# State-space side work in five lanes, eighteen groups of seven products, and cache products on GpSimd

## The chip, the cores and the metric

One core of a Trainium2 chip runs the whole program in one launch. The metric is the device time of that core in microseconds (us); lower is better. The kernel before takes 1260.09 us, the median of three runs (1259.04 to 1262.6). Engines: TensorE (PE in the profile, its weight loads PEld) multiplies matrices, VectorE (DVE) and ScalarE (ACT) do elementwise work, GpSimd (POOL) does some elementwise work and issues DMAs, SyncE (SP) issues most DMAs.

## The reference, cut to what matters

One step of a decoder layer with two branches: attention over a sliding window, and a diagonal state-space model (S5). 528 prompt tokens (16 meta tokens and 512) and 8 sample tokens go through the same weights.

```python
h = rmsnorm(x) @ w_in                    # 2048 -> 8704 columns
q, k, v, z_a, u, z_s, g_a, g_s = split(h)   # 1024, 256, 256, 1024, 1024, 1024, 2048, 2048
o = window_attention(rope(norm(q)), rope(norm(k)), v)  # 16 query heads on 4 key heads, window 128
# state space: 64 groups of 16 channels, 64 complex states each
bu = b_bar @ u                           # per group and token
h_t = lam_bar * h_(t-1) + bu_t           # scan over the tokens
y = gelu(real(c @ h) + d * u);  y = y * sigmoid(y @ w_glu + b_glu)
br_a = (o * silu(z_a)) @ w_attn_out
br_s = (y * silu(z_s)) @ w_ssm_out
out = x + (sigmoid(g_a) * br_a + sigmoid(g_s) * br_s) @ w_out
```

For each sample token attention runs over a cache of 16 meta and 127 window positions and the token itself: scores are a product of the cached keys with the query, summed over 64 dimensions; the output is a product of the cached values with the weights, summed over 144 positions. Updated caches and states are outputs too. All is float32.

## The kernel before, in words

**Products.** A float32 product is made from split operands: each weight unit (128 x 1024) is loaded as `raw`, rounded by ScalarE to `whi`, and VectorE computes the remainder `wlo` (L1019 and L1020); a product is whi·xh + whi·xl + wlo·xh, three matmuls for each 128 rows. The 536 token columns are held in two halves of 268, of which gates and queries use 260. A *block* is 128 output columns of `w_in` for all tokens: two weight units, 16 row tiles, three matmuls and two column halves, 96 matmuls (`mm`, L1168).

A *group* (`quad`, L1419, with `Quads` for its weights) makes two blocks from seven half-sized products instead of eight, by forming sums of weight units on VectorE (L1084) and sums of inputs (`tau`) once: 7 x 8 x 3 = 168 matmuls instead of 192. `NQ` says how many groups there are, and `NA` how many plain blocks stand ahead of them. `XORDER` and `ORDER1` fix the order of the 48 gate blocks (g_s, z_s, z_a, g_a) and of the u, k and v blocks.

**Order of the program.** Start with norms and five blocks; four plain blocks; `NQ` groups (four of them, `QHEADS`, make the queries); the ordered blocks of `ORDER1` ("x" a gate block, "u" one eighth of u, "h" one of the four k and v blocks); the gate blocks left over (`while nx < 47`, L1719); gate block 47 by hand; eight half-blocks of the gated unit product, w_glu on Y1 (L1746); sixteen half-blocks of the state-space output product on Y2 (L1762); `bg.drain()`; the attention-output product on A (L1780); w_out in groups.

**Side work.** Everything else is written as generators and put into `Background` (L963). The products call `bg.step(budget)` after every few row tiles (`GRAIN` 2 in the state-space stage, so a step is 12 matmuls; 4 in attention, 24 matmuls). A step adds budget to a credit; the generators are run in turn, lane by lane; what they yield is taken off the credit (roughly us of VectorE), and `yield None` takes the lane out for the rest of this step, so that a later instruction is issued a step later. With `fair` off (in attention) the first lane runs as long as it can and the others get the rest. This fixes the order of the program; the framework then orders each engine's queue by its own estimate of times, with weight splits and evictions at high priority. Matmuls of side work are issued behind the last product (`issue_after`).

**State-space stage.** It begins with the first "u" block. Lane 1 runs `ssm_consts` for eight units (128 channels each): scaled copies on ScalarE, four tables on VectorE, and at its end the tap product `kp` whose result goes through memory into the matrices T (L417 to L427). Lane 0 runs `ssm_block` for each unit: the bu product (L478), its products with the table straight out of PSUM into p1 and p2 (L492, L493), the combination, the scan, the way back, and the output product (L534, L537), then the gelu and six stores to `yD` (L556). The loads of U (12 DMAs, `ssm_load`) are issued on GpSimd's queue when a unit is done.

**Attention.** `attention()` follows in lane 0 when the eighth unit is done: values, keys, then for 4 key heads a rope of the queries and 4 blocks each of scores, softmax, transposes and weighing. The sample tokens are a lane of their own, added at that point: `sample_heads` gathers their rows, `sample_weigh` loads the key cache and the value cache in 16 pieces each (`cache`, two buffers), multiplies each piece by the query or the weights and sums it, both on VectorE (L659, L660). Last, `Attn.sample` loads that output and the gate (`zs`, in the tile `dV` of attention, L922), transposes and multiplies them into `oT`; then `attended()` splits `oT` into the operands A of the attention-output product (L1712).

## Time and profile before

| | us |
|---|---|
| median of three runs | 1260.09 |
| lowest and highest | 1259.04, 1262.6 |
| the profiled execution's own time | 1259.92 |
| its span in the trace | 1258.1 |
| TensorE busy | 1245.8 |
| VectorE busy | 986.4 |
| ScalarE busy | 632.5 |
| GpSimd busy | 324.4 |

A row of the views names line, engine, operation, output and inputs by the program's names, shapes and count, then the busy time, the mean duration in ns, and the idle time of the engine before it with what ended it. A matmul's recorded duration (283 ns for 260 columns) overlaps the next; what counts is how many start in a stretch. A wait is put down to what came last. The chain of waits runs backwards from the last instruction, so its rows are the work that set the time.

### The profile page before, as it was taken

Reading aid. Unit: us, or ns where it says so; the run is one execution under the profiler, and the core shown is the slowest. Engines: PE = TensorE matmul, PEld = TensorE weight load, DVE = VectorE, ACT = ScalarE, POOL = GpSimd, SP = SyncE. Lnnn points to the kernel's source line nnn. Section 1 sums busy time; section 2 is a strip of 40 time slices with the busy share of each in tenths; the row PEclk is TensorE's granted clock in tenths of the full one; section 3 lists DMA queues with packets and bytes.
Section 4 is the critical chain, followed back from the end, with each engine's and each line's share of the span. In section 5 each row is a group of like instructions: output and inputs, shape, how many; then the busy total and the mean of one; then the engine's idle time right before and its main releaser. Section 6 shows DMA issues by size and latency. Waiting matters only on the chain.

```text
span 1258.1 us, 26470 instructions
## 1 busy us (share of the span) xinstructions
PE 1245.8 (99%) x10333; PEld 1221.6 (97%) x10333; DVE 986.4 (78%) x1516; ACT 632.5 (50%) x1351; POOL 324.4 (26%) x541
## 2 busy tenths in 40 slices
PE   9999999999999999999999999999999999999998
PEld 9999999999999999999999999999999899999998
DVE  8687878888898756778689858899987477887875
ACT  8554444444445587555552233657665433344342
POOL 0003999940000015337345132112111000000000
PEclk9999999999999999999999999999999999999999
DMA  8544443444464475557556479777667466555441
GB/s 294 198 162 149 138 144 110 143 127 162 153 195 154 144 241 175 176 167 180 170 145 173 124 232 278 244 218 230 215 201 240 151 195 190 166 186 168 143 138 51
DMA packets 99872, 222.42 MB, mean 177 GB/s; under 512 B 17324, under 2 KB 36868, under 8 KB 99716
## 3 DMA queue, kind: packets, MB, share of 16 engines
q1 hardware_dynamic: 86500, 191.97, 47.3%
q0 software_dynamic: 13248, 28.77, 8.9%
q8 instruction: 81, 1.33, 0.4%
q14 instruction: 43, 0.35, 0.1%
HBM read 183.17 MB, written 38.43 MB: 176 GB/s over the span
## 4 chain that ended last, share of the span: by engine, by line
PE 89%; issue 4%; DMA 3%; DVE 2%; POOL 1%; ACT 1%; SPq 0%; DVEq 0%; ACTq 0%; POOLq 0%
PE mm L1179 41%; PE pr L1415 37%; PE mm L1271 2%; PE wg L865 1%; PE aux L1415 1%; PE aux L1179 1%; DMA cache<-in_kc 1%; PE aux L1271 1%; DMA KH<-KH 1%; PE wg L537 1%; PE tr L537 1%; PE aux L816 1%; DMA qD<-x 1%; PE tr L478 0%; PE aux L817 0%
## 5 line engine op out<-in xcount | busy, mean ns | idle before, releaser
L1085 ACT CAST whi<-raw 128x1024 fp32r<-128x1024 f32 x168 | 173.2, 1049 | 167.8 <-DVE raw L1084 68.9
L1086 DVE TENSOR_TENSOR wlo<-raw,whi 128x1024 fp32r<-128x1024 f32 x168 | 206.7, 1251 | 56.4 <-ACT whi L1085 56.0
L1019 ACT CAST whi<-raw 128x1024 fp32r<-128x1024 f32 (+3 forms) x124 | 118.4, 964 | 147.1 <-PE mm L1179 70.7
L1415 PE MATMUL pr<-tau,whi 128*128 128x260 f32 x992 | 180.1, 283 | 0.0
L1179 PE MATMUL mm<-xh,whi 128*128 128x260 f32 (+1 forms) x744 | 172.8, 286 | 0.2 <-ACT xr L1244 0.2
L1179 PE MATMUL mm<-xh,wlo 128*128 128x260 f32 (+1 forms) x744 | 172.2, 285 | 0.0
L1179 PE MATMUL mm<-xl,whi 128*128 128x260 f32 (+1 forms) x744 | 171.8, 285 | 0.0
L1020 DVE TENSOR_TENSOR wlo<-raw,whi 128x1024 fp32r<-128x1024 f32 (+3 forms) x124 | 137.6, 1118 | 32.6 <-ACT whi L1019 32.1
L1415 PE MATMUL pr<-cb,whi 128*128 128x260 f32 x848 | 153.0, 283 | 0.0
L1415 PEld LDWEIGHTS pr<-tau,whi 128*128 128x128 f32 x992 | 152.7, 188 | 0.0
L1415 PE MATMUL pr<-tau,wlo 128*128 128x260 f32 x496 | 139.4, 282 | 0.0
L1415 PEld LDWEIGHTS pr<-cb,whi 128*128 128x128 f32 x848 | 130.8, 188 | 0.2 <-ACT z L1449 0.2
L1179 PEld LDWEIGHTS mm<-xh,whi 128*128 128x128 f32 x744 | 123.6, 188 | 1.6 <-issue 1.2
L1179 PEld LDWEIGHTS mm<-xl,whi 128*128 128x128 f32 x744 | 123.8, 188 | 0.4 <-issue 0.4
L1179 PEld LDWEIGHTS mm<-xh,wlo 128*128 128x128 f32 x744 | 123.4, 188 | 0.2 <-issue 0.2
L1084 DVE TENSOR_TENSOR raw<-raw 128x1024 f32<-128x1024 f32 x95 | 118.7, 1250 | 1.4
L1415 PE MATMUL pr<-cb,wlo 128*128 128x260 f32 x424 | 119.1, 283 | 0.2 <-DVE wlo L1086 0.2
L1415 PE MATMUL pr<-xl,whi 128*128 128x260 f32 x376 | 105.1, 282 | 0.0
L1415 PE MATMUL pr<-xh,wlo 128*128 128x260 f32 x376 | 105.0, 283 | 0.0
L1179 PE MATMUL mm<-Y,whi 128*128 128x260 f32 x576 | 104.4, 287 | 0.3 <-ACT t L1755 0.3
L1415 PE MATMUL pr<-xh,whi 128*128 128x260 f32 x376 | 104.3, 284 | 0.0
L1415 PEld LDWEIGHTS pr<-tau,wlo 128*128 128x128 f32 x496 | 93.1, 188 | 0.0
(432 smaller groups left out, 3022.9 us busy)
## 6 DMA issues: line engine op xcount, KB each, us to landing
raw<-in_w SPq DMA_DIRECT2D x202, 512.0 KB, 4.4
gD<-z SPq DMA_DIRECT2D x36, 260.0 KB, 3.1
t<-gD SPq DMA_DIRECT2D x32, 260.0 KB, 3.4
cache<-in_vc POOLq DMA_DIRECT2D x16, 286.0 KB, 3.4
cache<-in_kc POOLq DMA_DIRECT2D x15, 288.0 KB, 4.8
xr<-in_x SPq DMA_DIRECT2D x16, 268.0 KB, 6.0
xg<-in_x SPq DMA_DIRECT2D x8, 536.0 KB
sbw<-rawD SPq DMA_DIRECT2D x16, 260.0 KB, 6.8
```

Source lines behind the costliest of these rows:

```text
L537: nc.tensor.matmul(o[n], lhsT=D["CL"][:, 2 * e + n, i, 1:5], rhs=H[:, 2 * e + n, i, 0:140], start=False, stop=(i == 1))
L816: nc.tensor.matmul(ps[:, e, 0:272], lhsT=q, rhs=KH[:, k0:k0 + 272], start=True, stop=False)
L865: nc.tensor.matmul(pv[64 * e:64 * e + 64, 0:256], lhsT=V, rhs=pr[:, e::2], start=(i == 0), stop=(i == len(parts) - 1))
L1019: nc.scalar.copy(out=hi, in_=raw)
L1020: self.dve = nc.vector.tensor_tensor(out=lo, in0=raw, in1=hi.bitcast(F32), op=ALU.subtract).ins
L1084: nc.vector.tensor_tensor(out=o, in0=o, in1=i, op=ALU.add)
L1085: nc.scalar.copy(out=hi, in_=t)
L1086: self.dve = nc.vector.tensor_tensor(out=lo, in0=t, in1=hi.bitcast(F32), op=ALU.subtract).ins
L1179: m = nc.tensor.matmul(ps[:, c, 0:W], lhsT=wt[:, k], rhs=xo(kt, c), start=f, stop=l)
L1271: nc.tensor.matmul(ps[:, c, 0:260], lhsT=wt[:, kt % 8], rhs=xk(xo, kt, c, 8), start=f, stop=l)
L1415: m = nc.tensor.matmul(bank, lhsT=wt[:, p], rhs=x(p, e), start=first and f and p == 0, stop=l and p == 7, skip_group_check=not first and l ...
```

## The change: lanes, order, engines, groups

- `NQ` goes from 16 to 18. The order of the gate blocks follows it, so four blocks fewer are left for the loop ahead of block 47 (six instead of ten).
- `ORDER1` starts with two u blocks and ends with two x blocks.
- `Background` has five lanes, and its turn goes on where it stopped for want of credit. `BUDGET` falls from 6.4 to 5.6.
- The tap product and what follows leave `ssm_consts` for a generator of their own, `ssm_taps`, in lane 4. Loads of U and stores of y leave `ssm_block` for `transfers()`, in lane 2; a store is issued four steps after its unit.
- A wrapper `InOrder` keeps GpSimd's DMAs and products of this work in program order.
- bu is copied from PSUM by ScalarE into the place in `H` where the states come later, and VectorE multiplies from there with four wide products.
- The sample tokens' generator starts in lane 3 once the norms of the heads are known; its part on the caches waits for attention's keys, and it also runs `Attn.sample`, whose tile is now one of the cache's buffers.
- The products of cache pieces go to GpSimd; the sums stay on VectorE, a step later. The copy of the sink into `S` goes from GpSimd to ScalarE.
- Attention also waits for all units and their stores; `NDELAY` goes from 4 to 6 steps.

```diff
+class InOrder:
+    def __init__(self, tc, nc):
+        self.tc, self.nc, self.gpsimd = tc, nc, self
+    def dma_start(self, **kw):
+        return self.tc.keep_in_program_order(self.nc.gpsimd.dma_start(**kw))
+    def tensor_tensor(self, **kw):
+        return self.tc.keep_in_program_order(self.nc.gpsimd.tensor_tensor(**kw))
...
 def ssm_consts(...):
-    D["CL"] = CL
+    D["CL"], D["tab"] = CL, tab
     yield 1.4
+    behind(ssm_taps(nc, pool, dram, R, D, ub, bb, CL, e32, d_skip, later))
+
+def ssm_taps(nc, pool, dram, R, D, ub, bb, CL, e32, d_skip, later):
     yield None
+    yield None
+    while "kp" not in R:
+        yield None
...
     nc.gpsimd.dma_start(out=kD, in_=k0)
+    yield 0.3
+    yield None
+    yield None
     for j in range(4):
         nc.gpsimd.dma_start(out=R["T"][ub % 2]...)
...
+    R["ready"] = ub
 def ssm_block(...):
+    Hu = H[:, :, :, 9:9 + NC]
...
-                v.tensor_tensor(out=p1[:, i, a], in0=bi, in1=bc(tab[:, 0, a], 2, NB), op=ALU.mult)
-                v.tensor_tensor(out=p2[:, i, a], in0=bi, in1=bc(tab[:, 1, a], 2, NB), op=ALU.mult)
+                nc.scalar.copy(out=Hu[:, a, i], in_=b[:, :, 0:NC])
...
-        yield 2.2
+    yield 0.6
+    for i in range(2):
+        for j, p in ((0, p1), (1, p2)):
+            v.tensor_tensor(out=p[:, :, i], in0=hu[:, :, i], in1=bc(tab[:, j], 2, NB), op=ALU.mult)
+        yield 1.4
...
+    def store():
...
+    R["ys"].append([store, 4 if ub < 7 else 1])
 def sample_heads(...):
+    for _ in range(4):
+        yield None
 def sample_weigh(...):
-            v.tensor_tensor(out=t, in0=t, in1=by, op=ALU.mult)
+            nc.gpsimd.tensor_tensor(out=t, in0=t, in1=by, op=ALU.mult)
+            yield None
             v.tensor_reduce(out=out[:, c * n:(c + 1) * n], in_=t, axis=AX.X, op=ALU.add)
-            yield 1.5
-            for _ in range(CWAIT):
-                yield None
+            yield 0.8
 class Attn:
-        nc.gpsimd.tensor_copy(out=S[:, :, 144], in_=C["sink"][:, 4 * kv:4 * kv + 4])
+        nc.scalar.copy(out=S[:, :, 144], in_=C["sink"][:, 4 * kv:4 * kv + 4])
...
-        o = pool.tile([P, 2, 64], F32, name="o_s", tag="sv")
+        o = pool.tile([P, 576], F32, name="ozs", tag="cache")
+        zs = o[:, 128:192].rearrange("p (b c j) -> p b c j", b=8, c=2)
+        o = o[:, 0:128].rearrange("p (n d) -> p n d", n=2)
...
-        zs = pool.tile([P, 8, 2, 4], F32, name="zs", tag="dV", bufs=1)
...
-BUDGET = 6.4
+BUDGET = 5.6
-NDELAY = 4
+NDELAY = 6
-NA, NQ = 4, 16
+NA, NQ = 4, 18
-ORDER1 = [(k, 0) for k in "xuhuhuhuhuxuxuxu"]
+ORDER1 = [(k, 0) for k in "uuxuhuhuhuhuxuxx"]
 class Background:
-        ways = list(self.lanes)
+        n = self.first if self.fair else 0
+        ways = self.lanes[n:] + self.lanes[:n]
...
-                if not q or self.credit <= 0:
+                if self.credit <= 0:
+                    self.first = [w is q for w in self.lanes].index(True)
+                    break
+                if not q:
                     continue
...
+    def transfers():
+        nonlocal loaded
+        S["ys"] = []
+        while loaded < 7 or done < 8 or S["ys"]:
+            ub = loaded + 1
+            for y in S["ys"]:
+                y[1] -= 1
+            if S["ys"] and S["ys"][0][1] < 0:
+                S["ys"].pop(0)[0]()
+            elif ub in uDs and ub < done + 2:
+                yield None
+                yield None
+                ssm_load(pn, S["U"][ub % 2], uDs.pop(ub))
+                loaded = ub
+            yield None
     def ssm(ub):
-        while ready < ub:
+        while min(S.get("ready", -1), loaded) < ub:
             yield None
...
     def finish():
             normed.append(1)
+            bg.add(samples(), lane=3)
     def samples():
+        for _ in range(6):
+            yield None
         qk = yield from sample_heads(...)
         smp.extend(qk)
+        while not (at and at.keyed):
+            yield None
         smp.extend((yield from sample_weigh(...)))
+        while not at.gated(3):
+            yield None
+        yield from at.sample(smpl, smp[2])
+        smp.append(True)
...
+            bg.add(transfers(), lane=2)
...
     def attention():
-        while not normed:
+        while not normed or done < 8 or S["ys"]:
             yield None
...
-        bg.add(samples(), lane=2)
...
+        at.keyed = True
...
-        while len(smp) < 3:
+        while len(smp) < 5:
             yield None
-        yield from at.sample(smp[2])
```

More of the change, by code (lines that the diff above doesn't have):

```diff
@@ L334, in ssm_states, with ssm_consts @@
     yield 2.5
-def ssm_consts(nc, pool, dram, R, D, ub, a_bT, a_bN, a_cT, e32, d_skip, later, free):
+def ssm_consts(nc, pool, dram, R, D, ub, a_bT, a_bN, a_cT, e32, d_skip, later, free, behind):
     v = nc.vector
@@ L940 @@
 NUNIT = 176
-CWAIT = 1
 GRAIN = 2
-BUDGET = 6.4
+BUDGET = 5.6
 GBUDGET = 0.5
@@ L1308, in trunk @@
     sp, Ds = None, {}
-    ready, done, uDs = -1, 0, {}
+    loaded, done, uDs = -1, 0, {}
+    pn = InOrder(tc, nc)
     def ssm_sets():
-        nonlocal ready
         for ub in range(8):
             Ds[ub] = {}
-            yield from ssm_consts(nc, sp, dram, S, Ds[ub], ub, A["bT"], A["bN"], A["cT"], e32, dsk,
-                                  lambda: tc.issue_after(bg.last), lambda: ub - 2 not in Ds)
-            ready = ub
-    def load_u():
-        for ub in sorted(uDs):
-            if ub < done + 2:
-                ssm_load(nc, S["U"][ub % 2], uDs.pop(ub))
+            yield from ssm_consts(pn, sp, dram, S, Ds[ub], ub, A["bT"], A["bN"], A["cT"], e32, dsk,
+                                  lambda: tc.issue_after(bg.last), lambda: ub - 2 not in Ds, lambda g: bg.add(g, lane=4))
+    def transfers():
[13 more added lines that the diff above has]
+            yield None
     def ssm(ub):
         nonlocal done
-        while ready < ub:
+        while min(S.get("ready", -1), loaded) < ub:
             yield None
-        yield from ssm_block(nc, sp, S, Ds[ub], ub, yD[ub], lambda: tc.issue_after(bg.last))
+        yield from ssm_block(pn, sp, S, Ds[ub], ub, yD[ub], lambda: tc.issue_after(bg.last))
         del Ds[ub]
         done = ub + 1
-        load_u()
     rawD = dram.tile([12, 2, P, 2, CH], F32, name="rawD")
@@ L1367, in sums @@
             else:
-                if "ax" not in S:
-                    S["ax"] = aux.tile([P, 2, 512], F32, name="aux")
                 ps = S["ax"][:, 1, P:]
@@ L1613, in trunk @@
                 nc.gpsimd.memset(t, 0.0)
-            S["ax"] = S.get("ax") or aux.tile([P, 2, 512], F32, name="aux")
-            S["bu"] = [aux.tile([P, 512], F32, name=n) for n in ("tr", "wg")] + [S["ax"][:, 0]]
-            S["kp"] = S["ax"][:, 1, 0:P]
             bg.add(ssm_states(nc, sc, sp, S, A["h0"]), lane=1)
             bg.add(ssm_sets(), lane=1)
+            bg.add(transfers(), lane=2)
             grain[0] = GRAIN
@@ L1623, in trunk @@
             v.tensor_tensor(out=uf, in0=ps, in1=R_, op=ALU.mult)
+        if n == 0:
+            S["ax"] = aux.tile([P, 2, 512], F32, name="aux")
+            S["bu"] = [aux.tile([P, 512], F32, name=nm) for nm in ("tr", "wg")] + [S["ax"][:, 0]]
+            S["kp"] = S["ax"][:, 1, 0:P]
         uD = dram.tile([P, 2 * CH], F32, name="uD", bufs=8)
-        nc.gpsimd.dma_start(out=uD, in_=flat(uf))
+        pn.dma_start(out=uD, in_=flat(uf))
         uDs[n] = uD
-        load_u()
         bg.add(ssm(n))
@@ L1654, in attention @@
         nc.gpsimd.memset(C["neg"], NEG)
-        at = Attn(nc, ap, aux, dram, C, oT, gD[24:32], rawD, rkD, rqD, lambda: tc.issue_after(bg.last))
+        at = Attn(pn, ap, aux, dram, C, oT, gD[24:32], rawD, rkD, rqD, lambda: tc.issue_after(bg.last))
         vals = [at.values(e) for e in range(2)]
```

47 lines of the change are left out of this document (25 added, 22 removed).

## Prediction

> **What bounds the kernel now.** I read the page's busy line and its chain first, then the busy time by stage, then the chain in order of time.
>
> ```profile
> PE 1245.8 (99%) x10333; PEld 1221.6 (97%) x10333; DVE 986.4 (78%) x1516; ACT 632.5 (50%) x1351; POOL 324.4 (26%) x541
> PE 89%; issue 4%; DMA 3%; DVE 2%; POOL 1%; ACT 1%; SPq 0%; DVEq 0%; ACTq 0%; POOLq 0%
> ...
> 113.40:437.50 324.10, 324.10 (x2700) 321.31 (x2699) 275.18 (x309) 155.06 (x219) 146.62 (x202) 1.00 0.45 146
> 437.50:740.00 302.50, 302.50 (x2559) 298.27 (x2558) 224.89 (x441) 161.10 (x495) 128.32 (x245) 1.00 0.59 171
> 740.00:999.50 259.50, 253.70 (x2065) 238.17 (x2064) 207.97 (x395) 147.71 (x402) 47.88 (x85) 1.00 0.73 228
> 999.50:1092.20 92.70, 92.65 (x770) 92.50 (x771) 69.27 (x90) 33.32 (x38) 0.19 (x1) 1.00 0.58 181
> ```
>
> In the stage rows the columns after the length are TensorE, its weight loads, VectorE, ScalarE and GpSimd, then granted clock, DMA share, GB/s. TensorE is the bound everywhere, at clock 1.00. The stages are: groups of seven products (113.4 to 437.5), ordered blocks with the state-space work (to 740), attention under the remaining products (to 999.5), then the attention-output product. Only 740 to 999.5 has visible TensorE idle: 259.50 - 253.70 = 5.8 us. So a gain must come from fewer matmuls or from those 5.8 us; a loss comes if side work no longer ends under its cover.
>
> ```profile
> 327.65 20.35 PE pr L1415 x168
> ...
> 992.05 0.91 POOL zs L924
> 995.41 2.73 DMA zs<-gD
> 998.82 0.63 ACT A L1698
> 999.55 92.65 PE mm L1179 x768
> ```
>
> ```profile
> 999.55 1.20 PE L1179 MATMUL mm<-A,whi 128*128 128x260 f32 x6 [2.43 <-ACT A L1698]
> ```
>
> The first row is one whole group, the last the plain product without side work: 92.65 / 768 = 0.1206 us a matmul. Between them is the end of the side work: the sample rows' gate `zs` loads only after attention's last weighing, and the split of A waits for it; TensorE stands 2.43 us.
>
> **Term 1, eighteen groups.** A group replaces two plain blocks: 2 x 96 x 0.1206 = 23.16 us against 20.35, so 2.81 saved; two more groups save 5.6 us. Their extra weight sums lie on VectorE, which the group stage leaves 49 us idle in 324 while TensorE never stops; I cost them at nothing. Were that cover short, it would show as idle in the stage that now has none.
>
> **Term 2, less cover.** Groups now end near 437.5 + 2 x 20.35 = 478, and four plain blocks (46.3 us) leave the stretch in which side work runs. Its end, now the last product before 996.9, moves to about 991.4. So 559 us of cover become 513. What must fit:
>
> ```profile
> L1020 DVE TENSOR_TENSOR wlo<-raw,whi 128x1024 fp32r<-128x1024 f32 x79 | 96.4, 1221 | 27.2 <-ACT whi L1019 26.7
> L659 DVE TENSOR_TENSOR cache<-cache,qv 128x576 f32<-128x576 f32 x16 | 12.1, 755 | 4.1 <-DMA cache<-in_kc 4.0
> L659 DVE TENSOR_TENSOR cache<-cache,ssc 128x572 f32<-128x572 f32 x16 | 11.6, 749 | 0.0
> L1216 DVE TENSOR_TENSOR z<-mm,R 128x520 f32<-128x520 f32 x14 | 9.7, 693 | 4.6 <-PE mm L1179 4.6
> L498 DVE TENSOR_TENSOR w<-p,p 128x528 f32<-128x528 f32 x8 | 5.6, 705 | 0.0
> L1768 DVE SCALAR_TENSOR_TENSOR z<-t,mm 128x520 f32<-128x520 f32 x16 | 11.1, 692 | 10.9 <-PE mm L1179 10.8
> L1222 DVE SCALAR_TENSOR_TENSOR z<-t,z 128x520 f32<-128x520 f32 x7 | 4.9, 693 | 0.0
> L492 DVE TENSOR_TENSOR p<-tr,tab 128x264 f32<-128x264 f32 x8 | 3.5, 432 | 14.9 <-PE tr L478 14.9
> L492 DVE TENSOR_TENSOR p<-wg,tab 128x132 f32<-128x132 f32 x8 | 2.3, 290 | 0.0
> ```
>
> VectorE in the two stages: 224.9 + 208.0 = 432.9 us. Off it come four blocks (each two splits and one eviction, 2 x 1.22 + 0.69 = 3.1; 12.5 in all), the 32 cache products (12.1 + 11.6 = 23.7), and the bu products: per unit six of 264 wide and four of 132 wide (6 x 0.432 + 4 x 0.290 = 3.75) become four of 528 (4 x 0.705 = 2.82), 7.4 over eight units. 389 us remain in 513: 76%, where 432.9 in 562 was 77%. On average the work fits as well as before. What decides is its division.
>
> *State-space stage.* A main block costs VectorE 3.1 to 3.8 us (a second L1222 eviction in half of them), about 0.245 per us of stage. 224.9 - 0.245 x 302.5 = 151 is side work, 18.9 a unit, 18.0 after. The code releases a step per 12 matmuls with 5.6 x 2/8 = 1.4 credits; a unit's declared costs are 19.8 (before 20.8 against 1.6, but three lanes waiting for one another needed some 17 steps). With five lanes it takes 14.1 steps, 14.1 x 12 x 0.1206 = 20.4 us, and about 6 us of its own matmuls (302.5 less 44 weight units of 48 matmuls, through eight): 26.4 us.
>
> ```profile
> 437.50:740.00 302.50, 52.98 (x44) 1.00 0.59 171
> ...
> L537 PE MATMUL tr<-H,CL x64: 280/282/284, 504.7 to 727.9; 128*128 128x140 f32 x64
> L865 PE MATMUL wg<-pp,V x48: 379/379/430, 814.5 to 992.2; 128*64 128x256 f32 x48
> ```
>
> (The first row is the stage's weight splits alone, L1020: 44.) Now a unit takes (727.9 - 504.7) / 7 = 31.9 us at 18.9/31.9 + 0.245 = 84% VectorE. After, 26.4 us would want 18.0/26.4 + 0.245 = 93%; at 84% it takes 30.3. With the same 55 us from the first u block to the first output product (449.1 to 504.7), the last unit reaches it at 478 + 55 + 7 x (26.4 to 30.3) = 718 to 745, and U of the last unit, loaded on short notice, adds up to some 8 us (12 issues of 0.55, rows below): 718 to 753. I take 738, 10 us later than now.
>
> *Attention.* Main work there is the 35 other splits (42.7) and some 54 operations of 520 columns at 0.69 as in L1216 (six plain evictions, sixteen of the state-space output product, four for each of eight gated pieces): 80 us in 259.5, 0.306 per us; side work 208 - 80 = 128. After: 128 - 24, plus contention.
>
> ```profile
> L1086 DVE TENSOR_TENSOR wlo<-raw,whi 128x1024 fp32r<-128x1024 f32 x44 | 56.4, 1305 | 17.7 <-ACT whi L1085 17.6
> ...
> L1086 DVE TENSOR_TENSOR wlo<-raw,whi 128x1024 fp32r<-128x1024 f32 x53 | 63.7, 1222 | 10.1 <-ACT whi L1085 10.1
> ...
> L241 POOL TENSOR_TENSOR work<-work 128x704 f32<-128x704 f32 x1 | 2.3, 2337 | 0.0
> L244 POOL TENSOR_TENSOR work<-work 128x384 f32<-128x384 f32 x1 | 2.0, 1988 | 0.0
> L242 POOL TENSOR_TENSOR work<-work 128x352 f32<-128x352 f32 x1 | 0.9, 944 | 0.0
> L811 POOL COPY S<-k_attc 128x4 f32<-128x4 f32 x16 | 10.3, 650 | 35.4 <-ACT Pn L838 25.2 <-DVE Pm L839 8.8 <-ACT S L820 1.4
> L641 POOL DMA_DIRECT2D cache<-in_kc x16 | 8.7, 543 | 64.1 <-DVE ssc L660 43.8 <-DVE m L829 10.9 <-DVE den L834 8.3
> ```
>
> The two splits are from 130 to 260, where GpSimd computes almost throughout, and from 275 to 435, where it is idle: 1305 against 1222 ns, 7%. A GpSimd product of 576 elements lies between the 352 and the 704 row, 0.9 to 2.3; I take 2.0 (beside busy VectorE), 64 us for 32, and 7% of that, 4 us, back onto VectorE. Side work 128 - 24 + 4 = 108. At the 80% load of this stage it takes 108 / (0.80 - 0.306) = 219 us (the same sum gives 259 now): 738 + 219 = 957, 937 to 972 at the bounds; if attention's own latency allows only 76%, 238 us, 956 to 991. All end before 991.4. The gate load no longer waits for the weighing (it moves into the cache tile), so I take the 2.43 us stall as gone: **-2.4**, bounds -2.4 and 0.
>
> The product puts a new wait ahead of each cache reduction on VectorE, with weight splits and softmax behind it; a `yield None`, 24 matmuls or 2.9 us, stands between them against 2.0 plus a load's landing. What is left is inside the next term.
>
> **Term 3, stalls elsewhere.** Of the 5.8 us, 3.4 are not at the end, most where the first scores wait:
>
> ```profile
> L816 PE MATMUL aux<-KH,QT x64: 283/288/400, 773.6 to 971.5; 128*128 128x272 f32 x64
> ...
>   PE aux L816: 2.0, 1
> ```
>
> (the second row is from the Q split, L800: who waited for it). A lighter VectorE could remove 3.4; a state-space stage at 90% could add as much, for side matmuls sit in TensorE's in-order queue with products behind them. I take +1.0, bounds -3.4 and +4.
>
> **Edits at nothing.** u first, with S["ax"] allotted later: u's eviction is the same instruction a block earlier. GpSimd kept in order: issues of 0.55 us behind one another; the store delayed four steps, and U, T, B loads queued behind it, wait less than the 5.8 us of those steps; the last unit is counted above. The sample heads' 14 loads and 12 stores move from attention into the state-space stage, past the U loads on that queue: 26 x 0.55 = 14 us more on an engine 128 us busy in 302, none of it ahead of a matmul that products wait behind. bu on ScalarE and the sink copy:
>
> ```profile
> L544 ACT ACTIVATE g<-tr 128x280 f32<-128x280 f32 x8 | 3.2, 404 | 20.8 <-PE tr L537 17.9 <-issue 2.8
> L422 ACT COPY k<-aux 128x96 f32<-128x96 f32 x8 | 1.9, 232 | 13.1 <-PE aux L417 13.1
> ```
>
> per unit three copies of 264 at 0.40 and two of 132 between 0.23 and 0.40, 1.8 us, on an engine 161 us busy in 302. Were it the late one, 8 x 1.8 = 14 us of unit latency, still ahead of 991.
>
> **Sum.** The profiled execution took 1259.92 us (span 1258.1), 0.2 below the median 1260.09. 1259.92 - 5.6 - 2.4 + 1.0 = 1252.9, on the median's scale **1253.1**. Bounds: -5.6 - 2.4 - 3.4 gives 1248.7; -5.6 + 0 + 4 gives 1258.5.
>
> **Rivals.** (a) *VectorE's relief goes further*: the 3.4 us of other stalls go too: the lower bound, 1248.7. For: 24 us off VectorE. Against: the state-space stage gets denser. (b) *The gain is eaten*: stalls of 4 us at 90% VectorE and an end of the old size: the upper bound, 1258.5. For: splits and side work share one in-order queue. Against: with 84% now, that stage has no visible idle. (c) *Slower: the state-space stage does not keep its pace.* If a unit takes longer than (991 - 219 - 533) / 7 = 34 us, that is if VectorE reaches under 18.0/34 + 0.245 = 77% there, attention ends behind its cover and TensorE stands before the attention-output product, 7 us for each further us of unit. It is slower from 8.0 + 3.8 us of new stall on, 35.7 us a unit. At 36, 1260.1 - 8.0 + 14 = 1266. For: the whole stage runs at 74% today. Against: 31.9 a unit is reached with more work and a looser release. (d) *GpSimd's products shut VectorE out for their whole length*: 64 us instead of 4, side work 168, 168 / 0.494 = 340 us, the end at 738 + 340 = 1078, 87 late: 1260.1 - 8.0 + 87 = 1339. Against: 7% in the row. The Trainium skill's GPSIMD Engine Reference, Key points, says that GpSimd shares its SBUF interfaces with VectorE and contends with instructions that have two SBUF inputs, as these splits do; by that rule alone VectorE gives time back, and the trace agrees, at 83 ns a split.
>
> **Chances.** Forecast 0.56, (a) 0.15, (b) 0.17, (c) 0.10, (d) 0.02. Likeliest case alone: 1249 to 1257. The range, to 8 in 10, takes in (a) and (b): 1247.5 to 1260. A measurement here can tell 0.3%, 3.8 us: faster is below 1256.3, so the forecast nearly whole, (a) and a little of (b), 0.71; same 0.18; slower 0.11.
>
> **What would show it.** Right: 10285 matmuls; groups ending near 478; the output products of the units spaced 26 to 31 us, the last one near 738; weighing over before 991; no idle ahead of the first A matmul; cache products near 2 us on GpSimd. Wrong: unit spacing over 34 us, an idle of more than 5 us ahead of A or at the first scores, or splits over 1.35 us while GpSimd multiplies.

## The result and the profile after

The changed kernel takes 1301.56 us (median of four runs, 1299.52 to 1303.3) where the kernel before takes 1261.12 in the same comparison: 1.0321 times as long, with a 95% interval of 1.0295 to 1.0347. It is 40 us slower; 1253.1 was predicted, 1247.5 to 1260 as the range. The profiled execution took 1299.52 us. One execution of the kernel before (2023.83 us) and one of a kernel with seventeen groups (1338.66 us) ran at a granted clock of 0.56 and 0.85 and are left out of the medians below.

The page of the kernel after, busy time by engine and the chain of waits:

```profile
PE 1255.3 (97%) x10285; PEld 1225.9 (94%) x10285; DVE 1006.7 (78%) x1456; ACT 651.4 (50%) x1421; POOL 362.0 (28%) x557
PE 76%; DVE 10%; DMA 7%; ACT 4%; issue 2%; POOL 1%; SPq 1%; DVEq 0%; ACTq 0%; POOLq 0%
```

There are 10285 matmuls instead of 10333, as the two groups should give, but TensorE's share of the chain has fallen from 89% to 76%. The busy time by stage (TensorE, its weight loads, VectorE, ScalarE, GpSimd, then granted clock, DMA share, GB/s) says where:

```profile
113.40:478.00 364.60, 364.60 (x3036) 361.82 (x3035) 307.22 (x342) 173.77 (x246) 146.83 (x202) 1.00 0.44 145
478.00:790.00 312.00, 310.37 (x2625) 306.30 (x2624) 225.03 (x395) 171.85 (x536) 130.91 (x247) 1.00 0.57 166
790.00:1039.00 249.00, 213.63 (x1611) 192.97 (x1609) 196.65 (x348) 137.60 (x405) 82.65 (x98) 0.95 0.72 221
1039.00:1131.80 92.80, 92.77 (x770) 92.57 (x771) 68.05 (x89) 32.41 (x37) 0.21 (x1) 1.00 0.54 164
```

The group stage is full to its end, and nearly the same holds up to 790. Between 790 and 1039 TensorE stands 249.0 - 213.6 = 35.4 us, and the attention-output product begins at 1039.0 instead of 999.5 before and 992.5 in the forecast (999.5 less 5.6 and 2.4, plus 1.0). The side work's own milestones are the state-space output products (first row, by line) and the weighings of attention (second row, by tile):

```profile
L569 PE MATMUL tr<-H,CL x64: 280/282/283, 540.8 to 786.3; 128*128 128x140 f32 x64
```

```profile
L902 PE MATMUL wg<-pp,V x48: 379/379/689, 891.8 to 1037.1; 128*64 128x256 f32 x48
```

The units are (786.3 - 540.8) / 7 = 35.1 us apart, where they were 31.9 by the same count (from the first product of the first unit to the last of the last, so both are 0.3 us too long). The mean hides one long gap: the first six gaps are 31 to 35 us, the last is 42. From the last output product to the last weighing pass 250.8 us, where it was 264.3. The products end before that. The end of the chain, in order of time and without the pieces under 0.2 us, is attention alone:

```profile
1035.17 0.70 DVE po L888
1036.01 1.53 PE wg L902 x12
1037.63 0.50 DVE oT L907 x2
1038.35 0.63 ACT A L1755
1039.03 6.04 PE mm L1220 x46
```

In the state-space stage no engine but TensorE is full: VectorE has 225.0 of 312 us, 72%. Two waits of the units can be seen; the experiments weigh them. First ScalarE's queue, here as a timeline in the middle of the stage (start, duration, line, output and input, count, and in brackets the idle time before):

```profile
579.77 2.03 ACT L383 ACTIVATE ct<-c,kept 128x64 f32<-128x64 f32 x8 [0.70 <-DVE CL L426]
581.71 0.66 ACT L580 ACTIVATE g<-g 128x560 f32<-128x560 f32 x1
582.27 2.49 ACT L383 ACTIVATE ct<-c,kept 128x64 f32<-128x64 f32 x10
584.66 1.03 ACT L1060 CAST whi<-raw 128x1024 fp32r<-128x1024 f32 x1
585.60 3.45 ACT L383 ACTIVATE ct<-c,kept 128x64 f32<-128x64 f32 x14
...
590.17 0.36 ACT L518 COPY H<-tr 128x264 f32<-128x264 f32 x1
...
593.38 0.27 ACT L518 COPY H<-wg 128x132 f32<-128x132 f32 x1
```

The new bu copy (L518) of a product that was done at 588.3 stands behind the scaled copies of the constants (L383), and the last of its five copies ends at 593.6. Second, the last unit. VectorE's timeline:

```profile
748.96 0.69 DVE L1263 SCALAR_TENSOR_TENSOR z<-t,z 128x520 f32<-128x520 f32 x1
753.58 1.23 DVE L1061 TENSOR_TENSOR wlo<-raw,whi 128x1024 fp32r<-128x1024 f32 x1 [3.92 <-ACT whi L1060]
758.40 0.70 DVE L1257 TENSOR_TENSOR z<-mm,R 128x520 f32<-128x520 f32 x1 [3.60 <-PE mm L1220]
759.29 1.23 DVE L1061 TENSOR_TENSOR wlo<-raw,whi 128x1024 fp32r<-128x1024 f32 x1 [0.19 <-ACT whi L1060]
765.04 1.23 DVE L1061 TENSOR_TENSOR wlo<-raw,whi 128x1024 fp32r<-128x1024 f32 x1 [4.53 <-ACT whi L1060]
768.02 0.17 DVE L520 TENSOR_TENSOR sst<-A,tr 128x16 f32<-128x16 f32 x1 [1.75 <-ACT H L518]
```

and GpSimd's queue at that time:

```profile
729.73 3.81 POOL L37 DMA_DIRECT2D U<-uD  x7 [0.23 <-DMA T<-kD]
742.31 4.06 POOL L37 DMA_DIRECT2D qD<-x  x8 [8.77 <-ACT x L650]
747.98 2.00 POOL L37 DMA_DIRECT2D kD<-x  x4 [1.61 <-DVE z L1257]
749.97 3.31 POOL L37 DMA_DIRECT2D yD<-g  x6
...
790.11 3.31 POOL L37 DMA_DIRECT2D yD<-g  x6 [35.56 <-DVE g L583]
```

U of the last unit is issued by 733.5, the gelu before it is done by 747.3, and for 18 us VectorE does nothing but the products' own work. The bu product of that unit runs at 766, and TensorE has no idle time ahead of it: products stand ahead of it in TensorE's queue, and that is its place there.

### The profile page after: what moved, and what is told of

It is laid out like the page before. It is cut to its first block, busy times and chain, and to the rows that moved or that the text cites. A ratio compares the mean times of both kernels' runs of the same rounds, so it can differ in the third digit from the quotient of the medians.

```text
span 1297.7 us, 26385 instructions
## 1 busy us (share of the span) xinstructions
PE 1255.3 (97%) x10285; PEld 1225.9 (94%) x10285; DVE 1006.7 (78%) x1456; ACT 651.4 (50%) x1421; POOL 362.0 (28%) x557
## 4 chain that ended last, share of the span: by engine, by line
PE 76%; DVE 10%; DMA 7%; ACT 4%; issue 2%; POOL 1%; SPq 1%; DVEq 0%; ACTq 0%; POOLq 0%
PE pr L1472 39%; PE mm L1220 31%; DVE wlo L1061 2%; DMA raw<-in_w 1%; PE aux L1472 1%; PE aux L1220 1%; DMA xr<-in_x 1%; DVE QT L837 1%; DMA z<-gD 1%; ACT S L869 1%; DMA sbw<-rawD 1%; DVE S L859 1%; ACT ct L383 1%; PE tr L569 1%; DMA rb<-rkD 1%
## 5 line engine op out<-in xcount | busy, mean ns | idle before, releaser
L1127 DVE TENSOR_TENSOR wlo<-raw,whi 128x1024 fp32r<-128x1024 f32 x182 | 223.6, 1249 | 65.5 <-ACT whi L1126 64.9
L1472 PE MATMUL pr<-tau,whi 128*128 128x260 f32 x1120 | 203.3, 283 | 0.0
L1472 PEld LDWEIGHTS pr<-tau,whi 128*128 128x128 f32 x1120 | 172.4, 188 | 0.0
L1472 PE MATMUL pr<-tau,wlo 128*128 128x260 f32 x560 | 157.5, 282 | 0.0
L1220 PE MATMUL mm<-xh,whi 128*128 128x260 f32 (+1 forms) x648 | 151.3, 286 | 1.9 <-DVE z L1257 1.6
L1220 PE MATMUL mm<-xl,whi 128*128 128x260 f32 (+1 forms) x648 | 150.7, 286 | 0.0
L1220 PE MATMUL mm<-xh,wlo 128*128 128x260 f32 (+1 forms) x648 | 149.9, 285 | 0.0
L1220 PEld LDWEIGHTS mm<-xh,whi 128*128 128x128 f32 x648 | 107.9, 188 | 2.7 <-DVE z L1257 2.0
L1220 PEld LDWEIGHTS mm<-xl,whi 128*128 128x128 f32 x648 | 108.2, 188 | 0.8 <-issue 0.8
L1220 PEld LDWEIGHTS mm<-xh,wlo 128*128 128x128 f32 x648 | 107.4, 188 | 0.6 <-issue 0.6
```

The source lines that it names most:

```text
L1127: self.dve = nc.vector.tensor_tensor(out=lo, in0=t, in1=hi.bitcast(F32), op=ALU.subtract).ins
L1220: m = nc.tensor.matmul(ps[:, c, 0:W], lhsT=wt[:, k], rhs=xo(kt, c), start=f, stop=l)
L1472: m = nc.tensor.matmul(bank, lhsT=wt[:, p], rhs=x(p, e), start=first and f and p == 0, stop=l and p == 7, skip_group_check=not first and l ...
```

## Experiments

The order of TensorE's queue is fixed when the program is built: side matmuls are traced behind a product, and the framework moves them further back to where its own estimate has their data ready. TensorE hardly stops before 790, so the place of a side matmul, counted in blocks of 96 products ahead of it, is its time. "Place" below means that count, of the 46 blocks that it has ahead of A with sixteen groups (44 with seventeen, 42 with eighteen); counted in the traces, the products give the same differences between kernels.

**Part by part: bu on ScalarE, GpSimd's order, the groups.** Four kernels, timed beside each other (before 1261.37).

bu straight from PSUM on VectorE again:

```diff
-                nc.scalar.copy(out=Hu[:, a, i], in_=b[:, :, 0:NC])
+                v.tensor_tensor(out=p1[:, i, a], in0=bi, in1=bc(tab[:, 0, a], 2, NB), op=ALU.mult)
+                v.tensor_tensor(out=p2[:, i, a], in0=bi, in1=bc(tab[:, 1, a], 2, NB), op=ALU.mult)
...
```

> The kernel after, with one part undone: bu goes again straight from PSUM into VectorE's products with the tables (six of 264 and four of 132 per unit), ScalarE copies nothing into H. Theory S (the ScalarE copies lengthen each unit: in the kernel after 7 to 12 us pass from the bu product to the last product with the tables, 2 to 6 before): the units' output products come every 27 to 30 us instead of 35.1, the last one near 740, time 1255 to 1275. Theory Q (GpSimd's fixed order holds back loads and stores, ScalarE's copies only fill a wait that is there anyway): the spacing stays 33 to 36 us and the time within 5 us of 1301. Theory C (the cover is simply 46 us too short for any version of this side work): the last output product moves, but the time stays above 1285.

1295.96 us, ratio 1.0276 (1.026 to 1.0291); units 33.6 us apart, the last output product at 777.3 instead of 786.3. So the copies cost 1.5 us a unit on average and 5.6 us of the 40; theory S has the right sign and about a fifth of the size it claimed. The units do not gain evenly: the first five gaps are 2.2 us shorter, then the gap ahead of the seventh unit is 51.6 us (31.4 in the kernel after) and the last one 22.5. The time stays above 1285, as theory C expected.

GpSimd's order left to the framework:

```diff
-        return self.tc.keep_in_program_order(self.nc.gpsimd.dma_start(**kw))
+        return self.nc.gpsimd.dma_start(**kw)
-        return self.tc.keep_in_program_order(self.nc.gpsimd.tensor_tensor(**kw))
+        return self.nc.gpsimd.tensor_tensor(**kw)
```

> The kernel after, with GpSimd's DMAs and products left to the framework's order again. Theory Q: the bu product of the last unit no longer stands 20 us behind its loads (747 to 767), the last output product comes at 765 or sooner instead of 784, and the time falls by 15 us or more, to 1287 or less. Theory S: the spacing of the units stays near 35 us, the time falls by less than 8 us, or rises, since the six stores and the sample heads' loads change places.

1293.57 us, 1.0257 (1.0242 to 1.0272). The last bu product comes at 755 instead of 768 and the last output product at 774.8; the first five gaps between units stay at 34 to 37 us, the last two are 29 and 26 (31 and 42 in the kernel after). Theory Q's event is there, worth 8.0 us instead of 15 or more.

Sixteen groups in the kernel after (`NQ = 16`):

> The kernel after with sixteen groups instead of eighteen: four plain blocks (46.3 us) more ahead of the end of the cover, 5.6 us more of products. Theory C: side work that is 40 us late finds its cover again, and the time comes back to 1258 to 1266. Theories S and Q as the only cause: the same return is expected, since the units are as slow as before but covered; they differ in that the output products of the units keep their spacing of 34 to 36 us here, with every wait between the units the same as in the kernel after.

1272.49 us, 1.0092 (1.0075 to 1.0109): 29 us come back, not 40. The spacing stays 35.0, and the last weighing is at 1007.8, 16 us later than before, so this side work overruns the old cover too, and theory C's 1258 to 1266 is missed.

Eighteen groups in the kernel before (`NQ = 18`), and nothing else:

> The kernel before with eighteen groups as the only edit. By the prediction's own sum (side work of 433 us on VectorE in 513 us of cover, less 10 us, at the pace of before): the last output product near 728 + 40 = 768, attention 259 us after it, its end near 1030 against a cover that ends at 991: 35 to 40 us of TensorE standing, time 1290 to 1298. If side work of before has slack that its credits hide, 1255 to 1270. Theory C (cover) thus expects slower than 1285, theories S and Q nothing of their own.

1296.6 us, 1.0282 (1.0266 to 1.0297). The two groups alone cost 35.2 us. Its rows for the output products, the weighing, and what waits at the end:

```profile
L537 PE MATMUL tr<-H,CL x64: 280/282/283, 544.7 to 767.0; 128*128 128x140 f32 x64
```

```profile
L865 PE MATMUL wg<-pp,V x48: 379/379/689, 869.8 to 1012.2; 128*64 128x256 f32 x48
```

```profile
1020.91 1.76 DMA oD<-o_s
...
1023.55 8.05 DMA o_s<-oD
...
1031.73 0.46 PE aux L930
```

Units are 31.8 us apart as before, only 39 us later, attention takes 245 us, and then the sample tokens' output goes through memory with nothing left to cover it. That the time lies within the expected 1290 to 1298 is in part luck: attention ended 18 us sooner than the 1030 of that sum, and the wait for the sample tokens' output, which the sum did not have, keeps TensorE standing 18.9 us. Before, the last weighing stood at 45.62 of 46 blocks: the side work ended 0.4 block, under 5 us, ahead of its cover. That is what "76% on average" did not show.

**Does attention's length follow VectorE's load?** Each timed once (before 1262.77 in that comparison). Fourteen of sixteen cache pieces left out:

```diff
-        for c in range(16):
-            t, more = more, load(c + 1) if c < 15 else None
+        for c in (0, 15):
+            t, more = more, load(15) if c < 15 else None
...
```

> The kernel after, with fourteen of the sixteen pieces of each cache left out (no load, no product, no sum; zeros stand in their place, so the sample tokens' attention is not computed): VectorE loses 28 sums of 0.74 us, 21 us, GpSimd 28 products, 42 us. Theory T, the prediction's (attention's length is its VectorE work over VectorE's free share, 108 us in 219): 21 us less work and 4 us less contention make it 51 us shorter; from the last output product to the last weighing 253 becomes near 202, TensorE no longer stands, time 1255 to 1262. Theory L (its length is a chain of steps that wait for one another, whatever the engines' shares): 243 to 253 remain, time 1285 to 1301.

1295.53 us. The cache products on VectorE again:

```diff
-            nc.gpsimd.tensor_tensor(out=t, in0=t, in1=by, op=ALU.mult)
+            v.tensor_tensor(out=t, in0=t, in1=by, op=ALU.mult)
```

> The kernel after, with the 32 cache products back on VectorE: 24 us more work there, 4 us less contention. Theory T: attention takes 20 / 0.494 = 40 us longer, 293 us from the last output product to the last weighing, time near 1340. Theory L: 248 to 262, time 1296 to 1310. Were GpSimd's products the thing that slows VectorE down (rival (d) of the prediction), the time would fall below 1290.

1292.5 us: faster than with the products on GpSimd, below theory L's range and above the 1290 that was set for rival (d). The stretch from the last output product to the last weighing in the three kernels (after, pieces left out, products on VectorE):

```profile
786.00:1037.00 251.00, 217.11 (x1642) 196.90 (x1643) 197.86 (x350) 138.43 (x406) 82.65 (x98) 0.95 0.72 222
```

```profile
787.00:1032.00 245.00, 218.62 (x1640) 198.17 (x1639) 164.46 (x323) 140.71 (x406) 27.95 (x42) 0.93 0.64 193
```

```profile
787.00:1030.00 243.00, 215.12 (x1645) 195.88 (x1643) 197.85 (x382) 140.35 (x406) 35.52 (x66) 0.95 0.75 230
```

VectorE's busy time is 164.5 to 197.9 us and the length 243 to 251: 33 us less work, 6 us less time. Theory T, which expected 202 and 293 us in these two kernels, falls. Even the 6 us need not be the work: the third kernel is 8 us shorter than the first with no less of it. The third row says something else as well: with 32 operations fewer VectorE was busy just as long (197.86 against 197.85). Groups of VectorE from 786 to 1040, first the kernel after (products on GpSimd), then products on VectorE:

```profile
L1061 DVE TENSOR_TENSOR wlo<-raw,whi 128x1024 fp32r<-128x1024 f32 x26 | 35.8, 1375 | 1.3 <-ACT whi L1060 1.1
L837 DVE TENSOR_TENSOR QT<-sbw,QT 64x512 fp32r<-64x512 f32 x16 | 14.6, 911 | 1.2 <-ACT QT L836 0.7
L865 DVE TENSOR_REDUCE m<-S 128x4 f32<-128x580 f32 x16 | 12.0, 749 | 0.2
L888 DVE TENSOR_TENSOR po<-tr,k_attc 128x512 f32<-128x512 f32 x16 | 10.9, 681 | 1.7 <-PE tr L884 1.7
L876 DVE TENSOR_TENSOR Pm<-S,den 128x64 f32<-128x64 f32 x16 | 8.9, 558 | 0.3
L866 DVE TENSOR_SCALAR m<-m 128x4 f32<-128x4 f32 x16 | 5.3, 329 | 0.1
```

```profile
L1061 DVE TENSOR_TENSOR wlo<-raw,whi 128x1024 fp32r<-128x1024 f32 x27 | 32.8, 1217 | 0.4 <-ACT whi L1060 0.2
L865 DVE TENSOR_REDUCE m<-S 128x4 f32<-128x580 f32 x16 | 12.0, 750 | 0.1
L888 DVE TENSOR_TENSOR po<-tr,k_attc 128x512 f32<-128x512 f32 x16 | 11.0, 686 | 3.4 <-PE tr L884 3.1
L837 DVE TENSOR_TENSOR QT<-sbw,QT 64x512 fp32r<-64x512 f32 x16 | 11.0, 686 | 1.2 <-ACT QT L836 0.7
L876 DVE TENSOR_TENSOR Pm<-S,den 128x64 f32<-128x64 f32 x16 | 3.5, 217 | 0.2
L866 DVE TENSOR_SCALAR m<-m 128x4 f32<-128x4 f32 x16 | 2.6, 166 | 0.1
```

With GpSimd multiplying, these operations with two inputs in SBUF get longer (911 for 686, 558 for 217, 1375 for 1217 ns), and the scaling of `m` too (329 for 166); the reduction and the product that reads PSUM do not change. 24 us of work went to GpSimd, where it takes 46 us (24.1 and 22.1 in its two groups), and about as much came back as longer operations, 16 us of it in the rows shown. The Trainium skill's SBUF — State Buffer, in "SBUF: two separate sides", says that VectorE and GpSimd hold one pair of ports in turn, for a whole instruction, and that VectorE needs it for two SBUF inputs or in a fast mode; these rows agree in which operations get longer, and the scaling of `m` would be of the second kind, which no run here separates.

**The constants' scaled copies off ScalarE.** In the kernel after, and in the kernel before, 32 copies of 0.25 us a unit became four products on GpSimd:

```diff
-        for k in range(4):
-            for a in range(4):
-                times(t[:, a, :, k], c[:, a], R["lamp"][:, r, k, 4 * ub + a:4 * ub + a + 1])
+        for i in range(2):
+            nc.gpsimd.tensor_tensor(out=t[:, :, i], in0=bc(c[:, :, i], 2, 4),
+                                    in1=bc(R["lamp"][:, r, :, ps].rearrange("p k a -> p a k"), 3, 32), op=ALU.mult)
...
```

> The kernel after, with the 32 scaled copies of the constants' tables t1 and t2 in each unit (0.25 us each, 8 us in ScalarE's queue, where the gelu of one unit and the bu copies of the next stand behind them) replaced by four products of 512 elements on GpSimd. Theory SQ (ScalarE's queue sets a unit's length): the output products come every 28 to 31 us instead of 35, the last one at 745 to 760, time 1265 to 1285. Theory Q (GpSimd's fixed order sets it): GpSimd gets some 5 us more per unit in its order, the spacing stays 34 us or more, time 1298 or more.

> The kernel before with the same edit alone. Theory SQ: its units, 31.6 us apart, come every 26 to 29 us, the last output product at 690 to 710 instead of 726, so that side work ends some 20 us ahead of its cover, and the time stays within 1257 to 1261, since only the stall of 2.6 us ahead of A can go. If credits and not ScalarE's queue set the units there: the spacing stays 31 to 32 us, same time.

1306.95 and 1281.72 us, each timed once: 5 us slower than the kernel after, 19 us slower than before. The units are 36.6 and 34.8 us apart. The first result is what theory Q expected (34 us or more, 1298 or more); the second fits neither expectation. Theory SQ is not confirmed, but the test isn't clean: GpSimd took 1.24 to 1.28 us for each product, so its queue grew by 5 us a unit. In the second kernel the last output product has its place at 28.8 blocks, where it is 27.6 before. What sets a unit's place in the framework's estimate stays open in this point.

**The place in the queue.** The sample tokens' rows gathered when attention starts, as before:

```diff
             normed.append(1)
-            bg.add(samples(), lane=3)
...
         bud[0] = BUDGET2
+        bg.add(samples(), lane=3)
```

> The kernel after, with the sample tokens' rows gathered again when attention starts instead of in the state-space stage. Theory E (a unit's pace is the place that the framework gave its side matmuls in TensorE's fixed queue, by its own estimate of when their data come; the engines wait for that place): in the queue as built only the last unit's matmuls move, its output product from 29.08 to 27.57 blocks of products; the other units keep their places. So the last output product comes 1.5 x 11.6 = 17 us earlier, near 767, the others within 2 us of the kernel after; attention then takes 247 to 256 us; time 1282 to 1292. Theory V (VectorE or ScalarE sets the pace, by what they have to do): all units move a little or none, the last by less than 8 us.

1289.32 us. Only the last unit moved, as its place said; the rows of its output products and weighing:

```profile
L569 PE MATMUL tr<-H,CL x64: 280/282/283, 540.6 to 768.6; 128*128 128x140 f32 x64
```

```profile
L902 PE MATMUL wg<-pp,V x48: 379/379/634, 878.9 to 1020.3; 128*64 128x256 f32 x48
```

17.7 us earlier at the output products and 16.8 at the weighing, with the same instructions; 10 to 12 of them reach the time, since the products end first and TensorE waits 4.3 us for the sample tokens' output behind the last weighing. What the gathering shifts in the framework's estimate, its 26 DMAs or its work on the other engines, was not taken apart.

**Three parts undone together**: bu by VectorE, GpSimd's order free, cache products on VectorE; the lanes, taps, u first and sample heads stay. With eighteen, seventeen and sixteen groups:

> The kernel after with three parts undone together: bu products by VectorE out of PSUM, GpSimd's order left to the framework, cache products on VectorE. Five lanes, taps in a lane of their own, u first, sample heads early, eighteen groups stay. Theory E: in the queue as built the last output product stands at 26.08 blocks instead of 29.08, so it comes 35 us earlier, near 750; with 245 to 255 us of attention behind it the last weighing falls at 995 to 1005 against products that end at 991, and the time is 1262 to 1272. Theory V: VectorE gets 24 + 7 us of work back, so the units are no faster than 33 us and attention longer: 1290 or more.

> The same three parts undone, with seventeen groups. Theory E with a fixed length of attention: last output product at 726 + (26.31 - 27.64) x 11.6 + 20.35 = 731, last weighing at 976 to 986, products end at 994 to 997: time 1254 to 1260, of which -2.8 from the group; the queue as built puts the last weighing right at the end of the products (44.0 of 44), so a tail of up to 5 us can be added. Theory C alone (any loss of cover is paid in full): 1260 - 2.8 + 23 = 1280.

> The same three parts undone, with sixteen groups. Theory E: the last output product at 726 - 1.56 x 11.6 = 708 (before: 726), the last weighing 955 to 970, some 1.1 blocks of products left behind it, so the stall of 2.6 us ahead of A can go: time 1255 to 1260, the same as before. What the lanes are worth then shows as cover that is not used. If the lanes themselves cost time elsewhere (stalls in the state-space stage): 1262 to 1270.

Measured beside each other (before 1261.38). The column "last unit" is the first output product of the last unit, 2 us ahead of the last one; "attention" runs from that last one to the last weighing, and "products" are the matmuls of the main products (L1217) in between:

```
groups  time us   ratio (95%)               place  last unit             last weighing  attention  products
18      1277.08   1.0122 (1.0100 to 1.0144)  26.08  751.7 (750 expected)  1013.6         260.0      1432
17      1265.44   1.0040 (1.0018 to 1.0062)  26.31  734.1 (731)           1002.2         266.1      1602
16      1257.64   0.9973 (0.9962 to 0.9984)  26.08  711.8 (708)            986.2         272.5      1712
```

The output products of the last unit come within 4 us of what the place gave, in all three. The time with eighteen groups is 5 us over the expected range, and that with seventeen 5 us over 1260, the size of the tail that was allowed for, because attention took 260 and 266 us, not the 245 to 255 assumed. Its length is not fixed either: the more products share TensorE's queue with it, the longer it gets, here 12.5 us for 280 products (34 us of TensorE), and in the kernel before 264 us with 1631 of them, against 245 with 1294 when it has eighteen groups. With sixteen groups side work ends 13 us ahead of A and the kernel is 0.27% faster than before.

The 40 us divide along these kernels into +35.2 for two groups alone; -19.5 (1277.1 - 1296.6) for the lanes and what goes with them; and +24.5 (1301.6 - 1277.1) for the three parts, of which each alone gave 5.6, 8.0 and 7 to 11. The -19.5 is not an earlier end of attention: its last weighing is at 1013.6 in the first row of the table and at 1012.2 in the kernel before with `NQ = 18`. The last unit is done 13 us earlier, but attention takes 15 us longer; what is gone is the tail, for the sample tokens' output is loaded at 947 instead of 1023, and A begins 1.9 us after the last weighing instead of 21.5.

**A step out of attention's chain.** The row maximum left out of the softmax, in the kernel after, and in the kernel with seventeen groups and three parts undone:

```diff
-        v.tensor_reduce(out=m, in_=S, axis=AX.X, op=ALU.max)
-        v.tensor_scalar(out=m, in0=m, scalar1=-0.125, scalar2=None, op0=ALU.mult)
...
-            nc.scalar.activation(out=S[:, r], in_=S[:, r], func=AF.Exp, bias=m[:, r:r + 1], scale=0.125,
+            nc.scalar.activation(out=S[:, r], in_=S[:, r], func=AF.Exp, bias=C["shift"], scale=0.125,
...
```

> The kernel after, with the search for the row maximum left out of the softmax (a fixed shift of 40 stands in its place: one reduction of 0.75 us and one scaling of 0.15 us less on VectorE for each of 16 blocks, and ScalarE's exponentials no longer wait for them; only rows whose largest score is far from that shift would lose accuracy). Theory L (attention is a chain of steps): each of the 16 blocks gets 1 to 2 us shorter, from the last output product to the last weighing 253 becomes 225 to 237, time 1274 to 1286. Theory T (VectorE's load) with the measured insensitivity: as much as the cache runs, 0 to 9 us, time 1292 to 1301.

> The kernel with seventeen groups and three parts of the change undone (bu by VectorE, GpSimd's order free, cache products on VectorE), and the row maximum left out of the softmax as well. Theory L: attention ends 10 to 25 us earlier than in that kernel (last weighing 1002), ahead of its products, which end at 994 to 997; in the queue as built it stands at 43.4 of 44 blocks. Time 1252 to 1257, the seventeenth group's 2.8 us then gained. Otherwise 1261 to 1266 as without this edit.

1281.97 us, timed once, 19.6 us less than the kernel after. The same stretch as above:

```profile
787.00:1020.00 233.00, 212.05 (x1643) 193.58 (x1641) 178.57 (x318) 141.43 (x406) 83.88 (x99) 0.96 0.78 234
```

233 us for 251: 18 us shorter for 17 us of VectorE work (12.0 + 5.3 in the rows of L865 and L866), where 33 us of it from beside the chain gave 6. Theory L holds in kind: what counts is the length of the steps that wait for one another, beside the products in the queue.

The kernel with seventeen groups then takes 1253.33 us, ratio 0.9933 (0.9916 to 0.9949), 8 us faster than before, at the price of a softmax with a fixed shift. Its weighing:

```profile
L896 PE MATMUL wg<-pp,V x48: 379/379/430, 837.9 to 987.1; 128*64 128x256 f32 x48
```

Side work ends at 987, and A begins at 994, when the products end. The kernel is 4.3 us faster than the one with sixteen groups above, which fits the 2.8 us of a group within the spread of the runs; no run has sixteen groups without the row maximum.

## Why the prediction was wrong

- *Term 1, eighteen groups, -5.6.* Its facts held: 10285 matmuls, a full group stage that ends near 478. Its other side, four blocks of cover less, was carried to term 2 and lost there.
- *Term 2, the step that failed: "What must fit", VectorE's time over its free share.* The state-space stage was to take 26.4 to 30.3 us a unit at 84% VectorE; it took 35.1 at 72%. The lanes alone did not bring it either: with the three parts undone units still come every 31.1 us. Attention was to take 108 / 0.494 = 219 us; it took 251, and still 245 with 33 us less VectorE work. Both lengths had been read as loads. A unit's length is set by the places of its matmuls in TensorE's queue, fixed at build time (the last unit came within 4 us of its place in the four runs that forecast it; why the framework chose a place is not known beyond the parts undone above); attention's by steps that wait for one another and by the products between them. In the kernel before, this side work ended under 5 us ahead of its cover. The sum 738 + 219 = 957 became 786.3 + 250.8 = 1037.1, with A at 1039.0 instead of 992.5, 46.5 us later. What follows A takes as long as before (260.5 and 260.4 us), so the forecast of 1252.9 for the profiled execution becomes 1299.4, and 1299.52 was measured.
- *The last unit*, "up to some 8 us" for U loaded on short notice: the place of its bu product moved by more, 12 and 18 us in two runs, and for reasons named as free: GpSimd kept in order (8.0 us of time) and the sample heads' rows gathered ahead of its loads and stores (10 to 12). The argument "none of it ahead of a matmul that products wait behind" asked what TensorE waits for, not what waits for its place on TensorE.
- *bu on ScalarE, at nothing, else 14 us of unit latency.* Measured 1.5 us a unit, 9.0 us at the last output product and 5.6 us of time. The bound of 14 (8 x 1.8) holds; the cover "still ahead of 991" was missing.
- *Cache products.* 2.0 us on GpSimd was too much (1.38 to 1.50), and +4 us of contention too little: 24 us. The splits alone gave that 4 (26 splits, each 158 ns longer); the rest is in other operations, such as the small ones of the softmax, which took twice as long or more. Rival (d), shutting VectorE out, was right in kind, at half of GpSimd's 46 us instead of all of it.
- *Term 3 and the 2.4 us stall.* A stall before A stayed (1.5 us), now behind the last weighing; the "+1.0" of other stalls became 35.4 us of TensorE standing between 790 and 1039.
- *Rival (c)* named what happened, with its threshold (over 34 us a unit) and a chance of 0.10. Its price was wrong for the same reason: with 219 us of attention 35.1 us a unit gives 1260.1 - 8.0 + 7 x 1.1 = 1260; with 251 the threshold itself is (991 - 251 - 533) / 7 = 29.6, below what the kernel before had. By the trace before alone, 728 + 40 + 264 lies 41 us past 991: keeping each length as measured, instead of scaling it by a load, would have given the right sign. That it also comes near the size is luck: the last output product came 18 us later than 768, and attention took 13 us less than 264.

## What to carry to other kernels

Where one engine's queue is full and fixed in order, side work has a length that no load of another engine gives; ask how far ahead of its cover it ends (here under 5 us of 560), and take nothing off the cover that the chain doesn't give back first. A stage's load over another engine's free share is no length: test it with work taken from beside the chain and from inside it (6 us for 33 against 18 for 17). Pinning a queue or moving transfers ahead of others shifts where the framework places the dependent matmuls, even if the other engines have time to spare; count those places in the built order before costing it at nothing.

## What was not expected of the hardware

GpSimd's products made two of VectorE's small operations two to two and a half times as long (217 to 558 ns, 166 to 329), so that moving 24 us of work freed nothing. The Trainium skill's Perfetto Trace Analysis, "Optimizing Scalar/DVE Operations", says that moving work between those two might not help; here it did not.

TensorE's granted clock fell where it had stood for a few us. Stretches of the kernel after:

```profile
800.00:820.00 20.00, 16.43 (x135) 15.84 (x133) 14.25 (x28) 8.73 (x20) 1.81 (x4) 1.00 1.02 319
820.00:840.00 20.00, 13.71 (x93) 13.50 (x94) 13.56 (x24) 6.43 (x13) 7.89 (x14) 0.83 1.15 293
```

At 13.7 us busy in 20 the clock is 0.83, at 16.4 in 20 still 1.00. TensorE's timeline in the second stretch, behind a stall and 5 us later:

```profile
823.79 1.24 PE L1220 MATMUL mm<-Y,whi 128*128 128x260 f32 x4 [6.52 <-ACT t L1812]
...
827.86 1.07 PE L1220 MATMUL mm<-Y,whi 128*128 128x260 f32 x4
...
829.01 0.41 PE L1220 MATMUL mm<-Y,whi 128*128 128x260 f32 x2
```

The first rows hold four products in 1.24 and 1.07 us, the last two in 0.41: up to 829 the products begin about 0.22 us after one another, from then on every 0.12 us. So part of the time lost is slower matmuls. From the end of the groups to A, TensorE stands 37.0 us (5.8 before), and its 4236 matmuls keep it busy for 524.0 us, where 556.2 before less 388 matmuls of 0.1206 us would be 509.4. Of the 46 us by which A is late, about 31 are thus more standing and about 15 are longer matmul records; those 15 are not all the clock, since the last matmul ahead of every stall is recorded at its full 0.28 us.
